# Phase one of a hybrid decoder layer: sums of squares in three groups, eps inside them, tile 1 scaled out of PSUM, tile 2's scaling ahead of tile 1's low half, constants loaded last

## The chip, the core and the metric

One core of a Trainium2 chip runs one program. The time is device microseconds (us) of one execution, and a kernel's time is the median of its runs. Differences between runs of one kernel are of the order of a per cent (the three runs of the kernel before lie between 311.09 and 315.16 us). The engines have names in the profile: PE is TensorE's matrix multiplication and PEld its weight loads, DVE is VectorE, ACT is ScalarE, POOL is GpSimd, and SP is SyncE, which issues nearly all DMAs (transfers) here.

## The reference, cut to what matters

One layer: an RMS norm of x, scaled and shifted by numbers that come from c, then a wide projection, two kinds of attention, an output projection and a gated residual. Only the first lines matter for the change:

```python
def rms_norm(x, gain):
    y = x * lax.rsqrt(jnp.mean(x * x, -1, keepdims=True) + EPS)
    return y * gain

# scale, shift, gate: c (after SiLU) @ W_ada
h = rms_norm(x) * (1 + scale) + shift      # 512 positions x 1024 features
q_a, k_a, v_a, z_a, q_b, ... = split(h @ W_in)
```

x has 512 positions (S) and 1024 features (D). EPS is 1e-6. The kernel holds x transposed, with features on the partitions: eight tiles of 128 features x 512 positions, `xT[0]` to `xT[7]`, views of one array `xTp`.

## The kernel before, in words

**Phase one** (the first 52 us of the span) makes h and multiplies it with the first 768 columns of W_in. All later phases use the same h.

*The head.* SP issues the loads in a fixed order: the eight x tiles, then for k = 0 to 3 the ada weights and the projection weights of tile k, then `rest` (constants that are first read after phase one). ACT squares each x tile as it lands (`sq`, line 347), DVE adds the squares of four tiles into one (line 349), and PE sums such a group over its partitions by a multiplication with a column of ones (`sums`, line 336: four matmuls of 128 x 128 with one column, each with a weight load of its own). There are two groups, tiles 0 to 3 and tiles 4 to 7. The four columns of `pr` in PSUM then hold the sums of squares of the 512 positions. DVE makes `sx` = sum / D + EPS from them (line 358) and `rx` = sx^(-1/2) by the classic integer trick and two Newton steps (`rsqrt`, lines 97 to 109). Four transposes on PE (line 368) turn rx into `rbp`, a tile of PSUM in which every partition holds the 512 factors, and ACT copies it to `rb` in SBUF (line 381). PE has little real work in this stage; `fillers` (line 317) are matmuls whose results are thrown away, and the table `ND` says how many stand where.

*The middle.* For tile k, `scaled` multiplies x by the factors on DVE (line 276, in place). `mod_pe`, `mod_col` and `mod_ab` (tiles 0 and 1) or `mod_rows` (tiles 2 to 7, a custom operation on DVE, line 226) make `AB`, the scale and shift of the tile's features. `h_high` on ACT makes `hh`, the high part of h, and `hf`, the whole of it (line 282; for tile 0 lines 379 and 382); `h_low` on DVE makes `hl` = hf - hh (line 285). `weights_high` on ACT and `weights_low` on DVE split the projection weights alike into `swh` (line 268) and `swl` (line 271). Then PE does `first_proj` in three passes, n = 0, 1, 2: hh with swh, hh with swl, hl with swh (lines 292 and 293). `new_tile(k)` is called in the middle of the passes of tile k - 1 and sets the order for tile k on DVE and ACT: hh and hf, the next tile's modulation, hl, the next tile's scaling, the next tile's weights.

*Order.* The order of instructions on each engine is that in which the code issues them; each engine runs its own list from front to back and waits where an input or a buffer isn't ready. Buffers rotate: `T2` hands out from a pool of 128 x 512 tiles, `sq`, `diag` and `hf` among them, and who gets a buffer waits for the last reader of its former content. `ps_pj` is a rotating pool of PSUM banks for `pr`, `pm`, `pc` and `rbp`. SP's loads of later phases are issued in the same way, when the buffers that they fill come free: at tile 4 `load_next` is called five times, which issues `w_kv_cmp` and `w_kv_sel` in halves among others.

Of the kernel before, what the change touches and what calls it, by code (L numbers as in the profile page):

```python
# [9 lines left out]
F32 = mybir.dt.float32  # L10
# [10 lines left out]
EPS = 1e-6  # L21
# [8 lines left out]
WAIT_L, WAIT_M = 4, (0, 8)  # L30
PER_A, PER_B = 3.6, (3.5, 1.6, 7)
NEAR = 256
ND = (11, (0, 0, 0, 0, 1, 1, 1, 1), (2, 0), 1, 1, 0, 3)
NR = 4
LW = 4
PE_MODS = 2
# [45 lines left out]
def hybrid_layer_kernel(ctx, tc, A, out):  # L82
# [11 lines left out]
    def T2(dt, name):  # L94
        return t2.tile([128, S], dt, name=name, tag="t2")

    def rsqrt(v, n):

        y = sm.tile([128, n], F32, name="n_y")
        t = sm.tile([128, n], F32, name="n_t")  # L100
        DVE.tensor_scalar(y.bitcast(I32), v.bitcast(I32), -0.5, float(MAGIC), op0=OP.mult, op1=OP.add)
        DVE.tensor_tensor(t, y, y, op=OP.mult)
        DVE.scalar_tensor_tensor(t, t, -0.375 * NEWTON[0], v, op0=OP.mult, op1=OP.mult)
        DVE.scalar_tensor_tensor(y, t, 0.375 * NEWTON[0] * NEWTON[1], y, op0=OP.add, op1=OP.mult)
        DVE.tensor_tensor(t, y, y, op=OP.mult)
        DVE.scalar_tensor_tensor(t, t, 64.0 / 9.0, v, op0=OP.mult, op1=OP.mult)
        DVE.scalar_tensor_tensor(t, t, -10.0 / 3.0, t, op0=OP.add, op1=OP.mult)
        DVE.scalar_tensor_tensor(y, t, 5.0, y, op0=OP.add, op1=OP.mult)
        return y
# [93 lines left out]
    def load_ada(k):  # L203
        t = ada_ring[:, k % NR]
        if k < PE_MODS:
            ada[k] = t.rearrange("p (a b c) -> p a b c", a=8, b=2)
            for e, n in ((0, 4), (4, 2), (6, 2)) if k == 0 else ((0, 4), (4, 4)):
                SP.dma_start(ada[k][:, e:e + n], A["w_ada_cols"][k][:, e:e + n])
        else:
            ada[k] = t.rearrange("p (a b) -> p a b", a=2)  # L210
            for e in range(2):
                SP.dma_start(ada[k][:, e], A["w_ada_rows"][k - PE_MODS][:, e])
# [57 lines left out]
    def weights_low(k):  # L270
        DVE.tensor_tensor(ws[k][1], wst[k], ws[k][0].bitcast(F32), op=OP.subtract)

    def scaled(k, by, parts=(slice(0, S),)):
        y[k] = xT[k]
        for c in parts:
            DVE.tensor_tensor(y[k][:, c], xT[k][:, c], by[:, c], op=OP.mult)
# [7 lines left out]
    def h_low(k):  # L284
        DVE.tensor_tensor(hl[k], hf[k], hh[k].bitcast(F32), op=OP.subtract)
# [10 lines left out]
    with in_order(tc) as begun:  # L296
# [8 lines left out]
        for k in range(NR):  # L305
# [1 line left out]
            if k == 0:  # L307
                SP.dma_start(bl, A["bias"])
            load_wst(k)
        SP.dma_start(rest, A["rest"])  # L310
        DVE.memset(scz, 0.0)


# [20 lines left out]
        def sums(acc, f, l):  # L334
            for tb in range(NB):
                PE.matmul(pr[:, tb:tb + 1], acc[:, tb * 128:(tb + 1) * 128], ones, start=f and tb == 0,
                          stop=l and tb == NB - 1, skip_group_check=True)

        for k in range(8):
            sq = stp.tile([128, S], F32, name="sacc") if k == 4 else T2(F32, "sq")  # L340
            if k % 4 == 0:
                sacc = sq
            fillers(ND[1][k], xT[k])
            if k == 4:
                sums(sacc_a, True, False)
            for n, c in enumerate(halves if k == 7 else [slice(0, S)]):
                ACT.activation(sq[:, c], xT[k][:, c], AF.Square)
                if k % 4:
                    DVE.tensor_tensor(sacc[:, c], sacc[:, c], sq[:, c], op=OP.add)
                if k == 7:  # L350
                    fillers(ND[2][n], sq[:, c])
            if k == 3:
                sacc_a = sacc
        sums(sacc, False, True)
        for e in range(2):
            ACT.activation(scrow[:, 512 * e:512 * e + 512], pj_q[e], AF.Copy)
        sx = con.tile([128, NB], F32, name="sx")
        DVE.tensor_scalar(sx, pr[:, 0:NB], 1.0 / D, EPS, op0=OP.mult, op1=OP.add)
        rx = rsqrt(sx, NB)
        DVE.tensor_scalar(prm1, prm[:, 8:16], 1.0, None, op0=OP.add)  # L360
        DVE.tensor_tensor(prmg[:, 0:8], prm1, prm[:, 24:32], op=OP.mult)
        DVE.tensor_scalar(prmg[:, 8:16], prm[:, 24:32], 0.5, None, op0=OP.mult)
# [15 lines left out]
        for c in halves:  # L378
            ACT.activation(hh[0][:, c], y[0][:, c], AF.Identity, bias=AB[:, 0, 1:2], scale=AB[:, 0, 0:1])
        ACT.copy(lsb[0:40, LINE - NEAR:LINE], pl)  # L380
        ACT.activation(rb, rbp, AF.Copy)
        ACT.activation(hf[0], y[0], AF.Identity, bias=AB[:, 0, 1:2], scale=AB[:, 0, 0:1])
        weights_low(0)
        scaled(1, rb)
        h_low(0)

        def new_tile(k):

            h_high(k, halves if k < 4 else (slice(0, S),))
            if k < 7:  # L390
                mod_rows(k + 1, (1,) if k == 1 else (0, 1))
            h_low(k)
            if k < 7:
                scaled(k + 1, rb)
                weights_high(k + 1)
                weights_low(k + 1)

        for k in range(8):
            if k + NR < 8:
                load_ada(k + NR)  # L400
                load_wst(k + NR)
            elif k == LW:
                for _ in range(5):
                    load_next()
            for n in range(3):
                first_proj(k, n)
                if k == 0 and n == 0:
# [703 lines left out]
```

## Time and profile before

| | before |
|---|---|
| median of 3 runs | 312.44 us (311.09 to 315.16) |
| profiled execution, its own time | 312.03 us |
| span of that execution | 309.4 us |
| granted TensorE clock, mean | 0.999 |
| PE, PEld busy | 302.0 us (98%), 255.2 us (82%) |
| DVE, ACT, POOL busy | 241.6 us (78%), 194.9 us (63%), 4.1 us (1%) |

The span runs from the first to the last instruction that the profiler recorded; the execution's own time is 2.6 us longer. Times in the rows below are us from the span's start, and the means of one instruction are ns. A row's bracket, such as `[0.71 <-ACT rb L381]`, says how long the engine stood idle ahead of it and which instruction ended that idle time; what stands left of `<-` in a name is the output, right of it are the inputs. A DMA row gives the kilobytes and the us from issue to landing. PE counts as busy also where it does the fillers.

### The profile page before, as it was taken

To read this page: it belongs to the slowest core of one execution; us is meant where nothing else is said; L and a number is where in the kernel's file an instruction comes from. 1 tells how busy PE (TensorE), PEld (TensorE's weight loads), DVE (VectorE), ACT (ScalarE), POOL (GpSimd) and SP (SyncE) were. 2 spreads that over 40 slices of the span, in tenths; PEclk is the share of its full clock that TensorE was granted. 3 is DMA by queue.
4 is the path that set the end of the run, shared out by engine and by line. 5 is a ranking of instruction groups with operands and counts; after the bars stand their busy time and mean duration, and the time that the engine had idled before them with its cause. 6 is when DMAs were issued, how large, how long until landed. Compare 5 with 4: busy or idle time off the path is not lost.

```text
span 309.4 us, 5849 instructions
## 1 busy us (share of the span) xinstructions
PE 302.0 (98%) x2119; PEld 255.2 (82%) x2119; DVE 241.6 (78%) x666; ACT 194.9 (63%) x472; POOL 4.1 (1%) x22
## 2 busy tenths in 40 slices
PE   8999999999999999999999999999999999999995
PEld 3678888788988999889887888888888888788885
DVE  5679998999967567898999999988789696544221
ACT  5686448668967675676936665869778877422000
POOL 0000000000000000000000000000000000000000
PEclk9999999999999999999999999999999999999999
DMA  7999969800390909170454004140420220254101
GB/s 252 382 407 408 406 202 251 307 0 0 117 328 13 293 4 263 45 271 2 154 182 158 20 2 138 65 138 3 136 71 0 68 70 2 68 172 135 68 34 68
DMA packets 28231, 44.11 MB, mean 143 GB/s; under 512 B 1787, under 2 KB 19612, under 8 KB 28204
## 3 DMA queue, kind: packets, MB, share of 16 engines
q1 hardware_dynamic: 26908, 41.57, 39.3%
q10 hardware_dynamic: 1296, 2.18, 2.3%
q8 instruction: 16, 0.26, 0.3%
q14 instruction: 11, 0.09, 0.1%
HBM read 41.61 MB, written 2.14 MB: 141 GB/s over the span
## 4 chain that ended last, share of the span: by engine, by line
PE 78%; DVE 11%; ACT 4%; DMA 3%; issue 1%; SPq 1%; DVEq 0%; ACTq 0%
PE pj L484 28%; PE po L949 8%; PE sq L292 8%; PE pj L474 8%; PE s L874 7%; PE pt L932 4%; PE skv L293 4%; PE pt L922 3%; PE s L603 3%; DVE qs L535 2%; DMA raw<-in_w_gate 2%; DVE raw L709 2%; DMA xTp<-in_xT 2%; DVE wl L177 1%; PE s L666 1%
## 5 line engine op out<-in xcount | busy, mean ns | idle before, releaser
L176 ACT ACTIVATE wh<-raw 128x512 fp32r<-128x512 f32 (+1 forms) x52 | 31.3, 635 | 18.0 <-PE pj L484 14.1
L474 PE MATMUL pj<-wl,hh 128*128 128x256 f32 (+1 forms) x128 | 36.8, 288 | 0.1
L474 PE MATMUL pj<-wh,hh 128*128 128x256 f32 (+1 forms) x128 | 37.0, 289 | 0.0
L474 PE MATMUL pj<-wh,hl 128*128 128x256 f32 (+1 forms) x128 | 36.5, 285 | 0.0
L177 DVE TENSOR_TENSOR wl<-raw,wh 128x512 fp32r<-128x512 f32 (+1 forms) x52 | 34.9, 690 | 1.8 <-ACT wh L176 1.7
L886 ACT ACTIVATE pp<-pp,nm 128x256 f32<-128x256 f32 (+2 forms) x48 | 29.3, 615 | 7.0 <-DVE nm L879 6.9
L484 PE MATMUL pj<-hl,wh 128*128 128x512 f32 x80 | 32.2, 402 | 0.0
L484 PE MATMUL pj<-hh,wl 128*128 128x512 f32 x80 | 32.0, 400 | 0.0
L484 PE MATMUL pj<-hh,wh 128*128 128x512 f32 x80 | 32.0, 400 | 0.0
L879 DVE CUSTOM_DVE_ANT_0 pp<-s,bias 128x256 f32<-128x256 f32 (+2 forms) x48 | 25.6, 553 | 4.1 <-PE s L874 3.6
L484 PE MATMUL pj<-yh,wl 128*128 128x512 f32 (+1 forms) x72 | 26.6, 370 | 0.0
L484 PE MATMUL pj<-yl,wh 128*128 128x512 f32 (+1 forms) x72 | 26.6, 369 | 0.0
L1037 DVE SCALAR_TENSOR_TENSOR fin<-pj,gate,xr 128x512 f32<-128x512 f32 (+1 forms) x9 | 6.2, 692 | 25.9 <-PE pj L484 25.9
L484 PE MATMUL pj<-yh,wh 128*128 128x512 f32 (+1 forms) x72 | 26.4, 371 | 0.0
L474 PEld LDWEIGHTS pj<-wl,hh 128*128 128x128 f32 x128 | 24.1, 188 | 0.6 <-DVE wl L177 0.3
L874 PE MATMUL s<-kTb,qs 128*128 128x256 f32 (+2 forms) x96 | 24.3, 356 | 0.0
L474 PEld LDWEIGHTS pj<-wh,hl 128*128 128x128 f32 x128 | 24.1, 188 | 0.2 <-issue 0.2
L474 PEld LDWEIGHTS pj<-wh,hh 128*128 128x128 f32 x128 | 24.1, 189 | 0.1
L907 DVE TENSOR_SCALAR pp<-pp,rr,grev 128x256 f32<-128x256 f32 (+2 forms) x48 | 21.0, 475 | 0.5
L933 ACT COPY ptT<-pt 128x384 f32<-128x384 f32 (+1 forms) x32 | 15.8, 528 | 6.0 <-PE pt L932 5.9
L534 ACT ACTIVATE qs<-pt 64x512 fp32r<-64x512 f32 x16 | 9.5, 592 | 13.4 <-PE pt L529 7.3
L484 PEld LDWEIGHTS pj<-hh,wh 128*128 128x128 f32 x80 | 15.1, 188 | 3.0 <-issue 0.2
(238 smaller groups left out, 721.4 us busy)
## 6 DMA issues: line engine op xcount, KB each, us to landing
ada_ring<-in_w_ada_rows SPq DMA_DIRECT2D x12, 512.0 KB, 7.2
raw<-in_w_cmp SPq DMA_DIRECT2D x8, 512.0 KB, 5.4
raw<-in_w_gate SPq DMA_DIRECT2D x8, 512.0 KB, 5.6
raw<-in_w_o SPq DMA_DIRECT2D x8, 512.0 KB, 4.2
wst_ring<-in_w_qkv_a SPq DMA_DIRECT2D x8, 384.0 KB, 7.7
xTp<-in_xT SPq DMA_DIRECT2D x8, 256.0 KB, 4.6
bias<-line_d SPq DMA_DIRECT2D x8, 256.0 KB, 4.1
raw<-in_w_q_b SPq DMA_DIRECT2D x4, 512.0 KB, 6.5
```

The source lines that it names most:

```text
L176: ACT.activation(wh, src, AF.Copy)
L177: DVE.tensor_tensor(wl, src, wh.bitcast(F32), op=OP.subtract)
L292: PE.matmul(pj_q[tb], lt, w[:, 0:512], start=f, stop=l, skip_group_check=True)
L293: PE.matmul(pj_kv[tb // 2][:, tb % 2, :], lt, w[:, 512:768], start=f and tb % 2 == 0, stop=l, skip_group_check=True)
L474: PE.matmul(bank[:, t * n:(t + 1) * n], h[:, tb * 128:(tb + 1) * 128], w[:, k % 2, :], start=k == 0 and m == 0, stop=k == 7 and m == 2)
L484: PE.matmul(bank, w, h[:, tok], start=k == 0 and m == 0, stop=k == 7 and m == 2)
L874: PE.matmul(ps, qs[h][:, 128 * i:128 * i + 128], k[:, hl_, lo:lo + w], start=hl_ == 0, stop=hl_ == 1)
L879: DVE.tensor_tensor_reduce(out=P[:, g, 0:w], in0=ps, in1=bt, scale=1.0, scalar=init, op0=OP.add, op1=OP.min, accum_out=nm[:, g:g + 1])
L886: ACT.activation(P[:, g, 0:e], P[:, g, 0:e], AF.Exp, bias=nm[:, g:g + 1], scale=-1.0, accum_out=dn[:, g:g + 1])
L907: DVE.tensor_scalar(v, v, rr[:, g:g + 1], gates[:, g, br:br + 1], op0=OP.mult, op1=OP.mult)
L933: ACT.copy(T[:, 0:nb, :], rev(pt[:, 0:nb * 128].rearrange("p (b q) -> p b q", b=nb)))
L949: PE.matmul(o[64 * g:64 * g + 64, 128 * i:128 * i + 128], vb[:, 64 * g:64 * g + 64], sl["T"][g][:, b, :], start=first_of and b == 0, stop= ...
```

## The change

Five things are changed, all in phase one and its loads.

1. *Groups.* The squares are summed in three groups, tiles 0 to 3, 4 and 5, 6 and 7, and PE sums each over its partitions when it is done, so there is a third call of `sums`. Each group starts in a buffer of its own.
2. *eps inside.* The addition of tile 1's squares to tile 0's also adds D * EPS / 128 to every element, which after the sum over 128 partitions is D * EPS. The step that made `sx` is gone; `rsqrt` reads `pr` in PSUM and has the factor D in its constants.
3. *Tile 1 out of PSUM.* DVE scales tile 1 by `rbp` in PSUM and no longer by `rb` in SBUF, and on ACT tile 0's `hf` goes ahead of the copy to rb.
4. *Tile 2 first.* In `new_tile(1)` tile 1's `hl` goes behind tile 2's scaling and weights.
5. *Loads and fillers.* `rest` is issued at tile 4, behind the two halves of w_kv_cmp, and no longer behind the weights of tile 3. The ada weights of tile 0 come in four pieces where there were three. The filler that stood in the middle of `mod_pe(0)` stands behind it.

```diff
--- before.py
+++ after.py
@@ -30,7 +30,7 @@
 WAIT_L, WAIT_M = 4, (0, 8)
 PER_A, PER_B = 3.6, (3.5, 1.6, 7)
 NEAR = 256
-ND = (11, (0, 0, 0, 0, 1, 1, 1, 1), (2, 0), 1, 1, 0, 3)
+ND = (11, (0, 0, 0, 0, 1, 1, 1, 1), (2, 0), 1, 0, 1, 3)
 NR = 4
 LW = 4
 PE_MODS = 2
@@ -94,16 +94,16 @@
     def T2(dt, name):
         return t2.tile([128, S], dt, name=name, tag="t2")
 
-    def rsqrt(v, n):
+    def rsqrt(v, n, times=1.0):
 
         y = sm.tile([128, n], F32, name="n_y")
         t = sm.tile([128, n], F32, name="n_t")
         DVE.tensor_scalar(y.bitcast(I32), v.bitcast(I32), -0.5, float(MAGIC), op0=OP.mult, op1=OP.add)
         DVE.tensor_tensor(t, y, y, op=OP.mult)
-        DVE.scalar_tensor_tensor(t, t, -0.375 * NEWTON[0], v, op0=OP.mult, op1=OP.mult)
-        DVE.scalar_tensor_tensor(y, t, 0.375 * NEWTON[0] * NEWTON[1], y, op0=OP.add, op1=OP.mult)
+        DVE.scalar_tensor_tensor(t, t, -0.375 * NEWTON[0] * times, v, op0=OP.mult, op1=OP.mult)
+        DVE.scalar_tensor_tensor(y, t, 0.375 * NEWTON[0] * NEWTON[1] * times, y, op0=OP.add, op1=OP.mult)
         DVE.tensor_tensor(t, y, y, op=OP.mult)
-        DVE.scalar_tensor_tensor(t, t, 64.0 / 9.0, v, op0=OP.mult, op1=OP.mult)
+        DVE.scalar_tensor_tensor(t, t, 64.0 / 9.0 / times ** 2, v, op0=OP.mult, op1=OP.mult)
         DVE.scalar_tensor_tensor(t, t, -10.0 / 3.0, t, op0=OP.add, op1=OP.mult)
         DVE.scalar_tensor_tensor(y, t, 5.0, y, op0=OP.add, op1=OP.mult)
         return y
@@ -204,7 +204,7 @@
         t = ada_ring[:, k % NR]
         if k < PE_MODS:
             ada[k] = t.rearrange("p (a b c) -> p a b c", a=8, b=2)
-            for e, n in ((0, 4), (4, 2), (6, 2)) if k == 0 else ((0, 4), (4, 4)):
+            for e, n in ((0, 2), (2, 2), (4, 2), (6, 2)) if k == 0 else ((0, 4), (4, 4)):
                 SP.dma_start(ada[k][:, e:e + n], A["w_ada_cols"][k][:, e:e + n])
         else:
             ada[k] = t.rearrange("p (a b) -> p a b", a=2)
@@ -307,7 +307,6 @@
             if k == 0:
                 SP.dma_start(bl, A["bias"])
             load_wst(k)
-        SP.dma_start(rest, A["rest"])
         DVE.memset(scz, 0.0)
 
 
@@ -336,27 +335,27 @@
                 PE.matmul(pr[:, tb:tb + 1], acc[:, tb * 128:(tb + 1) * 128], ones, start=f and tb == 0,
                           stop=l and tb == NB - 1, skip_group_check=True)
 
+        groups = []
         for k in range(8):
             sq = stp.tile([128, S], F32, name="sacc") if k == 4 else T2(F32, "sq")
-            if k % 4 == 0:
-                sacc = sq
+            if k in (0, 4, 6):
+                groups.append(sq)
+            sacc = groups[-1]
             fillers(ND[1][k], xT[k])
-            if k == 4:
-                sums(sacc_a, True, False)
+            if k in (4, 7):
+                sums(groups[k // 6], k == 4, False)
             for n, c in enumerate(halves if k == 7 else [slice(0, S)]):
                 ACT.activation(sq[:, c], xT[k][:, c], AF.Square)
-                if k % 4:
+                if k == 1:
+                    DVE.scalar_tensor_tensor(sacc, sacc, D * EPS / 128, sq, op0=OP.add, op1=OP.add)
+                elif sq is not sacc:
                     DVE.tensor_tensor(sacc[:, c], sacc[:, c], sq[:, c], op=OP.add)
                 if k == 7:
                     fillers(ND[2][n], sq[:, c])
-            if k == 3:
-                sacc_a = sacc
-        sums(sacc, False, True)
+        sums(groups[2], False, True)
         for e in range(2):
             ACT.activation(scrow[:, 512 * e:512 * e + 512], pj_q[e], AF.Copy)
-        sx = con.tile([128, NB], F32, name="sx")
-        DVE.tensor_scalar(sx, pr[:, 0:NB], 1.0 / D, EPS, op0=OP.mult, op1=OP.add)
-        rx = rsqrt(sx, NB)
+        rx = rsqrt(pr[:, 0:NB], NB, D ** 0.5)
         DVE.tensor_scalar(prm1, prm[:, 8:16], 1.0, None, op0=OP.add)
         DVE.tensor_tensor(prmg[:, 0:8], prm1, prm[:, 24:32], op=OP.mult)
         DVE.tensor_scalar(prmg[:, 8:16], prm[:, 24:32], 0.5, None, op0=OP.mult)
@@ -378,10 +377,10 @@
         for c in halves:
             ACT.activation(hh[0][:, c], y[0][:, c], AF.Identity, bias=AB[:, 0, 1:2], scale=AB[:, 0, 0:1])
         ACT.copy(lsb[0:40, LINE - NEAR:LINE], pl)
+        ACT.activation(hf[0], y[0], AF.Identity, bias=AB[:, 0, 1:2], scale=AB[:, 0, 0:1])
         ACT.activation(rb, rbp, AF.Copy)
-        ACT.activation(hf[0], y[0], AF.Identity, bias=AB[:, 0, 1:2], scale=AB[:, 0, 0:1])
         weights_low(0)
-        scaled(1, rb)
+        scaled(1, rbp)
         h_low(0)
 
         def new_tile(k):
@@ -389,19 +388,24 @@
             h_high(k, halves if k < 4 else (slice(0, S),))
             if k < 7:
                 mod_rows(k + 1, (1,) if k == 1 else (0, 1))
-            h_low(k)
+            if k > 1:
+                h_low(k)
             if k < 7:
                 scaled(k + 1, rb)
                 weights_high(k + 1)
                 weights_low(k + 1)
+            if k == 1:
+                h_low(k)
 
         for k in range(8):
             if k + NR < 8:
                 load_ada(k + NR)
                 load_wst(k + NR)
             elif k == LW:
-                for _ in range(5):
+                for n in range(5):
                     load_next()
+                    if n == 1:
+                        SP.dma_start(rest, A["rest"])
             for n in range(3):
                 first_proj(k, n)
                 if k == 0 and n == 0:
```

What the change moves on three engines follows, before and after apart. First PE in the head, from the fillers on the x tiles to the transposes of rx; `pj` stands for pr, pm and rbp, and `skv_125` is where the fillers write. Before:

```order
L317 MATMUL skv_125<-xTp 128x128
L336 MATMUL pj<-ones,sq 128x1 x4
L317 MATMUL skv_125<-xTp 128x128 x3
L317 MATMUL skv_125<-sq 128x128 x2
L336 MATMUL pj<-ones,sacc 128x1 x4
L317 LDWEIGHTS zero
L317 MATMUL skv_125<-zero 128x512
L236 MATMUL pj<-ada_ring,scz 32x256 x4
L317 LDWEIGHTS zero
L317 MATMUL skv_125<-zero 128x512
L236 MATMUL pj<-ada_ring,scz 32x256 x4
L368 MATMUL pj<-first,n_y 128x128 x4
```

The same place on PE, after:

```order
L316 MATMUL skv_125<-xTp 128x128
L335 MATMUL pj<-ones,sq 128x1 x4
L316 MATMUL skv_125<-xTp 128x128 x3
L335 MATMUL pj<-ones,sacc 128x1 x4
L316 MATMUL skv_125<-sq 128x128 x2
L335 MATMUL pj<-ones,sq 128x1 x4
L316 LDWEIGHTS zero
L316 MATMUL skv_125<-zero 128x512
L236 MATMUL pj<-ada_ring,scz 32x256 x8
L316 LDWEIGHTS zero
L316 MATMUL skv_125<-zero 128x512
L367 MATMUL pj<-first,n_y 128x128 x4
```

Four `sums` matmuls came in ahead of the two fillers on `sq`, and a filler moved from the middle of the ada matmuls (line 236) to behind them.

Second, ACT's squares of the x tiles 0 to 6 with the queues that each waits for (DMAHW: a transfer). Before:

```order
L347 ACTIVATE sq<-xTp 128x512 [waits DMAHW1_49]
L347 ACTIVATE sq<-xTp 128x512 [waits DMAHW2_49]
L347 ACTIVATE sq<-xTp 128x512 [waits DMAHW3_49]
L347 ACTIVATE sq<-xTp 128x512 [waits DMAHW4_49]
L347 ACTIVATE sacc<-xTp 128x512 [waits DMAHW5_49]
L347 ACTIVATE sq<-xTp 128x512 [waits DMAHW6_49]
L347 ACTIVATE sq<-xTp 128x512 [waits DMAHW7_49]
```

The same place on ACT, after:

```order
L348 ACTIVATE sq<-xTp 128x512 [waits DMAHW1_49]
L348 ACTIVATE sq<-xTp 128x512 [waits DMAHW2_49]
L348 ACTIVATE sq<-xTp 128x512 [waits DMAHW3_49]
L348 ACTIVATE sq<-xTp 128x512 [waits DMAHW4_49,PE_49]
L348 ACTIVATE sacc<-xTp 128x512 [waits DMAHW5_49,DVE_49,Activation_49]
L348 ACTIVATE sq<-xTp 128x512 [waits DMAHW6_49,DVE_49]
L348 ACTIVATE sq<-xTp 128x512 [waits DMAHW7_49,PE_49]
```

The squares are the same, but the buffers rotate otherwise, and four of the seven now wait for a second engine as well: tile 3's square for PE, which still reads that buffer's former content.

Third, DVE in the middle, from the scaling of tile 1 to the weights of tile 2, with its waits (`Activation` is ACT). Before:

```order
L276 TENSOR_TENSOR xTp<-xTp,rb 128x512 [waits DMAHW2_49,Activation_49]
L285 TENSOR_TENSOR hl_86<-hf,hh_78 128x512 [waits Activation_49]
L271 TENSOR_TENSOR swl<-wst_ring,swh 128x768 [waits DMAHW0_49,Activation_49]
L226 ISA ada_ring,AB<-ada_ring,scrow,first 128x1024 [waits DMAHW1_49]
L226 ISA AB 128x1
L261 TENSOR_TENSOR AB<-pj,first 128x1 [waits PE_49]
L262 SCALAR_TENSOR_TENSOR AB<-pj,prm_100,first 128x1
L226 ISA ada_ring,AB<-ada_ring,scrow,prmg 128x1024 [waits DMAHW2_49,DVE_49]
L226 ISA AB 128x1
L285 TENSOR_TENSOR hl_87<-hf,hh_79 128x512 [waits DVE_49,Activation_49]
L276 TENSOR_TENSOR xTp<-xTp,rb 128x512 [waits DMAHW3_49]
L271 TENSOR_TENSOR swl<-wst_ring,swh 128x768 [waits DMAHW3_49,Activation_49]
```

The same place on DVE, after:

```order
L276 TENSOR_TENSOR xTp<-xTp,pj 128x512 [waits DMAHW2_49,Activation_49]
L285 TENSOR_TENSOR hl_86<-hf,hh_78 128x512
L271 TENSOR_TENSOR swl<-wst_ring,swh 128x768 [waits DMAHW1_49,Activation_49]
L226 ISA ada_ring,AB<-ada_ring,scrow,first 128x1024 [waits DMAHW2_49]
L226 ISA AB 128x1
L261 TENSOR_TENSOR AB<-pj,first 128x1 [waits PE_49]
L262 SCALAR_TENSOR_TENSOR AB<-pj,prm_100,first 128x1
L226 ISA ada_ring,AB<-ada_ring,scrow,prmg 128x1024 [waits DMAHW3_49,DVE_49]
L226 ISA AB 128x1
L276 TENSOR_TENSOR xTp<-xTp,rb 128x512
L271 TENSOR_TENSOR swl<-wst_ring,swh 128x768 [waits DMAHW4_49,DVE_49,Activation_49]
L285 TENSOR_TENSOR hl_87<-hf,hh_79 128x512
```

Tile 1's scaling reads the factors from PSUM (`pj`) and still waits for ACT; the `hl` behind it, which reads `hf` from ACT, has no wait of its own any more. Tile 1's `hl` (hl_87) stands behind tile 2's scaling and weights.

## The prediction

> **What bounds the kernel now.** I read the page first, then busy times by stage (each row: stretch, its length, then busy us of PE, PEld, DVE, ACT and POOL with counts, granted clock, DMA share, GB/s), then who waits for whom in the first 52 us, then the rows of the places that the change touches.
>
> ```profile
> span 309.4 us, 5849 instructions
> 0.00:15.48 15.48, 13.60 (x74) 7.41 (x74) 9.40 (x34) 9.14 (x17) 0.76 (x6) 1.00 0.88 317
> 15.48:22.65 7.17, 7.17 (x53) 5.72 (x52) 5.52 (x10) 5.64 (x12) 0.00 (x0) 1.00 1.03 406
> 22.65:48.34 25.69, 25.69 (x143) 21.41 (x142) 24.91 (x39) 14.68 (x23) 0.00 (x0) 1.00 0.89 331
> PEld sq L292 <- DVE hl L285: 1.3, 4, 0.4
> 22.65 0.69 DVE L285 TENSOR_TENSOR hl<-hf,hh 128x512 fp32r<-128x512 f32 x1 [0.88 <-ACT hf L282]
> 24.27 0.40 PE L292 MATMUL sq<-swh,hl 128*128 128x512 f32 x1
> 28.49 0.39 PE L292 MATMUL sq<-swh,hl 128*128 128x512 f32 x1
> 37.04 0.50 PE L292 MATMUL sq<-swh,hl 128*128 128x512 f32 x1
> 45.38 0.70 DVE L285 TENSOR_TENSOR hl<-hf,hh 128x512 fp32r<-128x512 f32 x1
> 52.09 8.12 PE pj L484 x35
> 60.20 0.44 PE pt L547 x4
> ```
>
> After 52.09 the chain of waits is PE's own work (35 L484 matmuls without a pause, then L547), so what the change does to the time is what it does to the end of phase one, unless a transfer arrives late. That end hangs on DVE. From 22.65 to 48.34 DVE is busy for 24.91 of 25.69 us; PE shows no gap there, but it waits four times for `hl` (1.3 us in all), and where it doesn't wait its rounds are shorter: third passes (swh with hl) of tiles 1 and 2 start at 24.27 and 28.49, a round of 4.22, while the two from there to tile 4's (37.04) take 4.28 each. DVE's hl of tiles 1 and 6 start at 22.65 and 45.38: five rounds of 4.55. So PE catches up with DVE, and tile 6's hl (45.38 + 0.70 = 46.08) sets when PE goes into its last 52.09 - 46.08 = 6.0 us. The granted clock is 1.00 in all three stretches. The question is thus how much later or earlier DVE starts its unbroken run.
>
> **The head: squares to rx.**
>
> ```profile
> 5.57 1.88 PE L327 MATMUL sq<-diag,ones_sq 128*128 128x512 f32 x4
> L327 PE MATMUL sq<-diag,ones_sq 128*128 128x512 f32 x4 | 1.9, 592 | 0.0
> 5.35 1.37 ACT L347 ACTIVATE sq<-xTp 128x512 f32<-128x512 f32 x2 [0.31 <-DMA xTp<-in_xT]
> 7.80 2.03 ACT L347 ACTIVATE sq<-xTp 128x512 f32<-128x512 f32 x4
> 5.52 2.28 DVE L349 TENSOR_TENSOR sq<-sq 128x512 f32<-128x512 f32 x3
> 7.85 0.97 PEld L336 LDWEIGHTS pj<-ones,sq 128*128 128x128 f32 x8 [0.38 <-DVE sq L349]
> 9.57 0.52 PEld L317 LDWEIGHTS skv<-sq 128*128 128x128 f32 x4
> 10.53 0.97 PEld L336 LDWEIGHTS pj<-ones,sacc 128*128 128x128 f32 x8 [0.43 <-DVE sacc L349]
> 10.53 1.05 PE L336 MATMUL pj<-ones,sacc 128*128 128x1 f32 x8 [0.24 <-DVE sacc L349]
> 11.62 0.16 DVE L358 TENSOR_SCALAR sx<-pj 128x4 f32<-128x4 f32 x1 [0.81 <-PE pj L336]
> 11.82 0.17 DVE L101 TENSOR_SCALAR n_y<-sx 128x4 int32<-128x4 int32 x1
> 14.83 1.09 ACT L379 ACTIVATE hh<-xTp,AB 128x256 fp32r<-128x256 f32 x2 [0.37 <-DVE AB L262]
> ```
>
> Tile 3's square gets a wait for PE, which must have read the first diag (the first L327 product, two of the four matmuls in the row). The four follow each other every (1.88 - 0.59)/3 = 0.43 us, so the first product ends at 5.57 + 0.43 + 0.59 = 6.59. The two squares from 5.35 to 6.72 last 0.63 to 0.69 each, so tile 3's started near 6.06; now it starts near 6.63 and ends near 7.27, 0.55 later. Queued behind it on ACT are the other squares, whose tile landed late anyway (tile 4's began after an idle time, at 7.12), so they lose 0.15 only. The last of the three additions, which ended at 7.80, would start at 7.30 and end at 7.99. First `sums` then at 8.04, before 7.85: +0.19.
>
> From there PE's weight loads stand one after another, (0.97 - 0.19)/7 = 0.111 us apart, and nothing lies between: 8 of group one, 6 of the fillers on x, **8 new ones of group two**, 4 of the fillers on the squares make 26 x 0.111 = 2.89, so the last group starts at 10.93. Before, it started at 10.53, after 0.43 of idle time waiting for DVE: the new loads first fill that hole, and only the rest shows. DVE isn't the bound now, since group three needs one addition (tile 7's) where there were three: ACT's last square ended at 9.83 and ends about 0.15 later, and half a tile's addition behind it is done near 10.4. The sums end 0.40 later, at 11.98. What goes is `sx`: 11.82 - 11.62 = 0.20. So **rx and all that follows start 0.20 later**; without the square's wait it would be 0.0. The filler moved out of `mod_pe(0)` lets the ada product end earlier, but mod_col stands behind the transposes, which need rx: worth nothing. More pieces of ada weights: one DMA issue more on SP, its data not needed before that: nothing. hh of tile 0, at 14.83, moves to 15.03.
>
> **The middle: tile 1 out of PSUM, tile 2 ahead of tile 1's low half** (times as before, the 0.20 comes on top).
>
> ```profile
> 16.08 0.59 ACT L381 ACTIVATE rb<-pj 128x512 f32<-128x512 f32 x1
> 16.57 0.81 ACT L382 ACTIVATE hf<-xTp,AB 128x512 f32<-128x512 f32 x1
> 17.28 0.83 ACT L268 ACTIVATE swh<-wst_ring 128x768 fp32r<-128x768 f32 x1
> 21.54 1.08 ACT L282 ACTIVATE hf<-xTp,AB 128x256 f32<-128x256 f32 x2
> 22.52 0.83 ACT L268 ACTIVATE swh<-wst_ring 128x768 fp32r<-128x768 f32 x1
> 16.70 0.69 DVE L276 TENSOR_TENSOR xTp<-xTp,rb 128x512 f32<-128x512 f32 x1 [0.71 <-ACT rb L381]
> 17.41 0.69 DVE L285 TENSOR_TENSOR hl<-hf,hh 128x512 fp32r<-128x512 f32 x1
> 18.14 0.96 DVE L271 TENSOR_TENSOR swl<-wst_ring,swh 128x768 fp32r<-128x768 f32 x1
> 19.02 1.28 DVE L226 CUSTOM_DVE_ANT_0 ada_ring<-ada_ring,scrow,first 128x1024 f32<-128x1024 f32 x1
> 20.42 1.33 DVE L226 CUSTOM_DVE_ANT_0 ada_ring<-ada_ring,scrow,prmg 128x1024 f32<-128x1024 f32 x1
> 23.26 0.69 DVE L276 TENSOR_TENSOR xTp<-xTp,rb 128x512 f32<-128x512 f32 x1
> 23.86 0.95 DVE L271 TENSOR_TENSOR swl<-wst_ring,swh 128x768 fp32r<-128x768 f32 x1
> 24.73 1.28 DVE L226 CUSTOM_DVE_ANT_0 ada_ring<-ada_ring,scrow,first 128x1024 f32<-128x1024 f32 x1
> ```
>
> Before, tile 1's scaling starts at 16.70 because rb is done (0.71 of idle time ends there). The change is to free it of rb, but in the order of the changed kernel this scaling still waits for ACT, and the hl behind it has lost its own wait for ACT though it reads hf. That fits one reading only: ACT's rb copy and DVE's scaling read the same PSUM tile, the scaling is held until ACT's rb is through, and since hf stands ahead of rb now, hl is covered by the same wait. So hf takes rb's place (16.08 to 16.89), rb goes from 16.79 to 17.38 (ACT's instructions begin 0.10 ahead of the recorded end of the last), and the scaling starts at 17.41, not 16.70: **+0.71**. hl, which waited for hf before, follows 0.61 later (hl to scaling, 22.65 to 23.26) at 18.02, swl 0.60 behind it at 18.62 (ACT's swh for it still ends at 18.11). Before 18.14: +0.48, and what hangs on it gets that too: the modulation at 19.02 and 20.42, AB, and tile 1's hf (21.54 + 1.08 ends at 23.10 now) and swh of tile 2 (22.52, ends at 23.83).
>
> Here moving hl pays: DVE no longer sits for 0.88 waiting for hf, and does tile 2's scaling near 22.3. But swl of tile 2 needs that swh, and comes at 23.86 as before. Tile 1's hl, which used to be done by then, goes behind it at 24.73 and takes 0.61, so the next modulation starts at 25.34 where it started at 24.73: **+0.61**. From there DVE has no idle time up to tile 7, so all of it reaches tile 6's hl. PE gets tile 1's hl at 25.42, where its third pass began at 24.27: it stands for 1.15 us, but with rounds of 4.2 it would be at tile 6's third pass by 25.42 + 5 x 4.2 = 46.4, and DVE's hl is there at 46.08 + 0.61 = 46.7. DVE sets the end.
>
> [...]
>
> **The loads.**
>
> ```profile
> rest<-in_rest SPq DMA_DIRECT2D x1, 481.0 KB, 8.2
> raw<-in_w_kv_cmp SPq DMA_DIRECT2D x2, 512.0 KB, 9.8
> 51.35 0.22 DVE L422 TENSOR_TENSOR kg<-rest 128x64 f32<-128x64 f32 x1
> ```
>
> `rest` gives 481 KB back to a stretch where the DMA share is 1.03, but nothing on DVE, ACT or PE waits there for a transfer that it delays, so that gain is 0. In the new place it stands on SP behind a wait for PE (as read from the order, up to tile 4's third pass: 37.04 + 4.2/3 + 0.8, some 39.3), lands 8.2 later near 47.5, and is first read at 51.35 + 0.8 = 52.2: 4.6 us to spare, 3 even with the 9.8 us of w_kv_cmp. The w_kv_sel behind it waits for its buffers anyway. Cost 0.
>
> **The sum.** +0.20 and +0.61 make +0.81. On the profiled execution's own time, 312.03 (span 309.4 and 2.6 around it), that is 312.84; on the median of the runs shown, 312.44, it is 313.25. I take **313.1**, as the two frames differ by 0.4. Bounds of what the trace doesn't show: tile 3's wait between 0 and 0.20; the PSUM reads of rsqrt and scaling between -0.1 and +0.3 (sx out of PSUM took 0.16, its neighbour out of SBUF 0.17: I take 0); DVE's offset not passed on (0) or PE's 1.15 passed on whole (+1.35 in all). That makes 312.0 to 313.8 about the frames.
>
> **Rivals.**
>
> *It works as meant* (22%). The scaling isn't held by rb and runs beside ACT's hf. Then hl goes at 17.41 and everything to 21.75 as before; the scaling of tile 2 fills the idle time, swl comes when swh is done (23.35) at 23.38, hl at 24.25, the modulation at 24.86: +0.13. In the head, if PE's new loads run into the idle time and tile 3's square is not held, sums end as before and sx is saved: the best is -0.43 - 0.20 = -0.63. Together -0.5: 311.5 to 311.9. For it: the idle times 0.71, 0.88 and 0.43 are there to be taken. Against it: the waits in the order.
>
> *rest comes late* (6%, the other side). The point is 52.2: rest must land within 12.9 us of its issue. If it lands behind both halves of w_kv_cmp, 9.8 + 8.2 = 18 us, DVE's kg starts at 57.3, 5 us late, with all of DVE's work on keys and queries behind it. PE has 8.12 us of L484 before L547 needs it, so between nothing and 5 us reach PE: 313 to 318; with half of it 315.7. Against it: 8.2 us for this very load in the fuller stretch.
>
> [...]
>
> **Chances and range.** My forecast 62%, as meant 22%, rest late 6%, dearer reads 5%, 5% for what I don't see. The range, 311.1 to 315.0, takes in the forecast's bounds with the scatter of the runs, the rival as meant, and the lower half of a late rest. 2% either way, about what a measurement of this kernel can tell from no change, is 306.2 and 318.7: faster by that 1%, the same 97%, slower 2%.
>
> **What will show it.** Right: DVE's L276 of tile 1 starts as ACT's rb ends, near 17.6, behind hf; no idle time of 0.88 ahead of the hl; the first sums near 8.04 and no idle time of 0.43 ahead of the last; PE waiting about 1 us for tile 1's hl; L484 starting near 52.9; rest landing before 49. Wrong: the scaling starting beside hf; DVE idle in tiles 3 to 6, where the offset would be eaten up; a wait of kg for DMA; any of the early loads landing at other times than before, since they set the squares.

## The result, and the profile after

The changed kernel takes 313.52 us (median of 22 runs, 312.95 to 317.0), the kernel before 312.07 us (22 runs, 310.69 to 316.73). The ratio is 1.0067, with a 95% interval of 1.0044 to 1.009: slower by 0.7%. Forecast was 313.1, +0.8 us; the ratio makes it +2.1 us (1.4 to 2.8), the two medians alone +1.45. In some executions of every kernel here PE's mean granted clock is 0.995 or less (in profiles of such executions it stands at 0.50 for 3.4 to 10.3 us, from about 11 us on), so spans below are medians of the executions whose mean clock is 0.998 or more: 309.4 to 309.6 before (in each of four comparisons), 311.2 after. The profiled execution of the changed kernel took 313.45 us.

```profile
span 311.4 us, 5887 instructions
53.75 8.15 PE pj L488 x35
61.90 0.44 PE pt L551 x4
```

The first row is the page's, the other two are from the chain of waits. PE's work behind phase one starts at 53.75, where it started at 52.09, and lasts 8.15 us (8.12 before). So 1.66 of the 2.0 us by which the span grew arise in phase one. Next, who waits for whom in the first 53 us (total, times, longest):

```profile
ACT sq L348 <- PE sq L326: 1.5, 1, 1.5
DVE xTp L276 <- ACT rb L381: 1.5, 1, 1.5
DVE swl L271 <- ACT swh L268: 1.1, 1, 1.1
PEld sq L292 <- DVE hl L285: 1.2, 2, 1.1
```

The first and the third wait are new. The scaling's wait for rb was 0.7 us before, and PE's longest wait for `hl` was 0.4. The head, by the timeline of ACT, PEld, PE and DVE:

```profile
5.89 2.25 PE L326 MATMUL sq<-diag,ones_sq 128*128 128x512 f32 x4
7.33 0.63 ACT L348 ACTIVATE sq<-xTp 128x512 f32<-128x512 f32 x1 [1.54 <-PE sq L326]
8.73 0.97 PEld L335 LDWEIGHTS pj<-ones,sq 128*128 128x128 f32 x8 [0.56 <-DVE sq L352]
10.29 0.97 PEld L335 LDWEIGHTS pj<-ones,sacc 128*128 128x128 f32 x8
11.63 0.97 PEld L335 LDWEIGHTS pj<-ones,sq 128*128 128x128 f32 x8
12.73 0.16 DVE L101 TENSOR_SCALAR n_y<-pj 128x4 int32<-128x4 int32 x1 [2.12 <-PE pj L335]
14.10 0.16 DVE L108 SCALAR_TENSOR_TENSOR n_y<-n_t,n_y 128x4 f32<-128x4 f32 x1
15.79 1.09 ACT L378 ACTIVATE hh<-xTp,AB 128x256 fp32r<-128x256 f32 x2 [0.67 <-DVE AB L262]
```

Tile 3's square stands 1.54 us waiting for the diag product and starts at 7.33, not at 6.63. The first sums start at 8.73 (7.85 before). From there to the last group it is 2.90 us without a gap, as worked out (26 loads of 0.111). rsqrt starts at 12.73, 0.91 later than before. Its eight steps last 0.16 us as before and take 1.37 us from first to last start (1.39 before), so reading the sums out of PSUM costs nothing that these rows show. Now the middle, ACT's rows, then DVE's:

```profile
17.04 0.81 ACT L380 ACTIVATE hf<-xTp,AB 128x512 f32<-128x512 f32 x1
17.76 0.57 ACT L381 ACTIVATE rb<-pj 128x512 f32<-128x512 f32 x1
24.01 0.83 ACT L268 ACTIVATE swh<-wst_ring 128x768 fp32r<-128x768 f32 x1
18.37 0.69 DVE L276 TENSOR_TENSOR xTp<-xTp,pj 128x512 f32<-128x512 f32 x1 [1.48 <-ACT rb L381]
23.10 0.69 DVE L276 TENSOR_TENSOR xTp<-xTp,rb 128x512 f32<-128x512 f32 x1
24.88 0.96 DVE L271 TENSOR_TENSOR swl<-wst_ring,swh 128x768 fp32r<-128x768 f32 x1 [1.08 <-ACT swh L268]
25.75 0.69 DVE L285 TENSOR_TENSOR hl<-hf,hh 128x512 fp32r<-128x512 f32 x1
26.35 1.28 DVE L226 CUSTOM_DVE_ANT_0 ada_ring<-ada_ring,scrow,first 128x1024 f32<-128x1024 f32 x1
26.49 0.50 PE L292 MATMUL sq<-swh,hl 128*128 128x512 f32 x1 [0.73 <-DVE hl L285]
47.01 0.69 DVE L285 TENSOR_TENSOR hl<-hf,hh 128x512 fp32r<-128x512 f32 x1
47.76 0.51 PE L292 MATMUL sq<-swh,hl 128*128 128x512 f32 x1
```

Tile 1's scaling reads PSUM and still starts 0.04 us behind the end of rb. Tile 2's scaling fills idle time (23.10), but its swl then stands 1.08 us for swh. From tile 0's hh to the modulation of tile 3 it is 26.35 - 15.79 = 10.56 us; before it was 24.73 - 14.83 = 9.90. These 0.66 and the head's 0.9 (hh: +0.96) are there unchanged in tile 6's hl, 47.01 against 45.38.

### The profile page after: what moved, and what is told of

The parts are those of the page before. It is cut to its first block, busy times and chain, and to the rows that moved or that the text cites. A ratio compares the mean times of both kernels' runs of the same rounds, so it can differ in the third digit from the quotient of the medians.

```text
span 311.4 us, 5887 instructions
## 1 busy us (share of the span) xinstructions
PE 303.4 (97%) x2127; PEld 256.6 (82%) x2127; DVE 241.2 (77%) x664; ACT 194.8 (63%) x472; POOL 4.3 (1%) x22
## 4 chain that ended last, share of the span: by engine, by line
PE 81%; DVE 7%; DMA 6%; ACT 2%; issue 1%; SPq 0%; POOL 0%; DVEq 0%; ACTq 0%; POOLq 0%
PE pj L488 33%; PE pj L478 9%; PE s L878 8%; PE po L953 8%; PE sq L292 6%; PE pt L936 4%; PE pt L926 4%; PE skv L293 3%; DMA wst_ring<-in_w_qkv_a 3%; PE s L607 3%; DMA ada_ring<-in_w_ada_cols 2%; DVE qs L539 2%; DVE kTb L557 1%; DMA xTp<-in_xT 1%; PE s L670 1%
## 5 line engine op out<-in xcount | busy, mean ns | idle before, releaser
L883 DVE CUSTOM_DVE_ANT_0 pa<-s,bias,nsink 128x256 f32<-128x256 f32 (+1 forms) x32 | 14.3, 448 | 4.2 <-POOL pa L887 2.4
```

Source lines behind the costliest of these rows:

```text
L883: DVE.tensor_tensor_reduce(out=P[:, g, 0:w], in0=ps, in1=bt, scale=1.0, scalar=init, op0=OP.add, op1=OP.min, accum_out=nm[:, g:g + 1])
```

## The experiments

**The head.** Why tile 3's square waits for PE is not in the code. The section on the change puts it down to buffers that rotate, but the pool of T2 has 40 tiles (`NT2`), and tile 3's square is the 22nd that is asked for, so no rotation gives it a used one. What is left is the placement of tiles in memory: the square has been given bytes that the first diag (one of the two matrices, made from c, that PE multiplies at line 326) holds, and starts as its product ends. No run shows addresses; that it hangs on how long other tiles live, here on the late load of `rest`, is what the first experiment tests. It undoes that move.

```
+        SP.dma_start(rest, A["rest"])      # behind tile 3's weights
...
-                    if n == 1:
-                        SP.dma_start(rest, A["rest"])
```

> The changed kernel with the load of rest back in its old place. The memory is then laid out otherwise, and no square of an x tile waits for PE any more. Theory A (the head lost 0.9 us because tile 3's square waits for PE's diag product, whose buffer it got when rest moved away): first sums near 7.9 instead of 8.73, rsqrt's first step near 11.9 to 12.1 instead of 12.73, phase one ending near 53.0 instead of 53.75, time some 0.7 us below the changed kernel. Rival B (the third group's weight loads on PE cost it): rsqrt's first step stays near 12.7, time as the changed kernel. [...]

Ratio to before 1.0048 (1.0017 to 1.0078), span 310.4: 0.8 us less than the changed kernel. ACT and PEld in the head of this version:

```profile
6.26 0.63 ACT L349 ACTIVATE sq<-xTp 128x512 f32<-128x512 f32 x1 [0.52 <-DMA xTp<-in_xT]
7.93 0.97 PEld L336 LDWEIGHTS pj<-ones,sq 128*128 128x128 f32 x8 [0.53 <-DVE sq L353]
10.82 1.59 PEld L336 LDWEIGHTS pj<-ones,sq 128*128 128x128 f32 x8
```

The square waits for its own tile, the first sums start at 7.93, and all three groups' loads still follow without a gap (2.89 us to the last). The last row lasts longer, and rsqrt starts at 12.54, because the clock halves at 11.1 in this execution; at full clock, as in the rows of the changed kernel, rsqrt would come 1.10 us behind 10.82, at 11.9 by this estimate. The diag product ended early in this execution (6.25), so its rows alone would show little of the wait; the spans at full clock show it. So theory A holds for the 0.8 us. Rival B isn't out for the rest: the last sums start at 10.82 where they started at 10.53, of which eps gives back 0.20, and the span is still 1.0 above before, 0.66 of it from the middle. How the other 0.3 is made up is not shown.

The second leaves rest late and gives tile 3's square a tile of another pool.

```
-sq = stp.tile(..., name="sacc") if k == 4 else T2(F32, "sq")
+sq = stp.tile(..., name=f"own{k}") if k in (3, 4) else T2(F32, "sq")
```

> The changed kernel, but tile 3's square has a buffer of its own (as tile 4's has); rest stays late. Theory A: as with rest early, the first sums come near 7.9 to 8.1, rsqrt's first step near 12.0, phase one 0.7 us sooner than in the changed kernel, time -0.7 us. Rival B (three groups) and rival D (moving rest itself costs, by its transfer): no gain, rsqrt near 12.7 or the same end of phase one.

> The changed kernel with a buffer of its own for tile 3's square, once more, since its time was left open. Theory A (the head's 0.65 to 0.9 us is the wait for the diag product): first sums near 7.9 to 8.1 and rsqrt near 11.9 to 12.1, modulation of tile 3 still 10.56 us behind tile 0's hh, time -0.6 to -0.8 us against the changed kernel, as with rest early. Rival E (PE's own late end of the diag products, not the square's wait, sets the first sums): first sums near 8.3 to 8.5, gain 0.3 us or less.

A miss: ratios 1.0102 (1.0065 to 1.0138) and 1.006 (1.0022 to 1.0098), span 311.2 in the second (six executions), no gain. PE and ACT in the head of the second:

```profile
3.76 2.34 PE L316 MATMUL skv<-zero 128*128 128x512 bf16 x5
8.52 0.63 ACT L348 ACTIVATE own<-xTp 128x512 f32<-128x512 f32 x1 [1.71 <-PE sq L326]
```

Tile 3's square is free now, but tile 4's waits for the last diag product, until 8.52. All of them read `ones_sq`, so tile 4's own tile seems to lie on its bytes; addresses are not shown here either. The edit moved the wait by one tile, and theory A isn't tested by it. It does bear on rival E, by a later row of PE:

```profile
8.48 0.95 PE L335 MATMUL pj<-ones,sq 128*128 128x1 f32 x8
```

The first sums start at 8.48 without idle time ahead of them, as rival E says (8.3 to 8.5). Where the diag products end late, PE itself comes late to the sums. In the changed kernel's profile PE's weight loads also stood idle for 0.56 us ahead of 8.73, waiting for the squares. Without that they would have started at 8.17, which is still 0.32 later than before. So the wait of the square is the larger part of the delay there, and PE's own lateness the rest.

The third makes this wait alone: the kernel before, with tile 3's square written into the first diag.

```
-sq = stp.tile(..., name="sacc") if k == 4 else T2(F32, "sq")
+sq = stp.tile(..., name="sacc") if k == 4 else dg[0] if k == 3 else T2(F32, "sq")
```

> The kernel before with one thing changed: tile 3's square is written into the first diag's buffer, so it waits for PE's first diag product; two groups, rest early, all else as before. Theory A (this wait is the head's loss): first sums start 0.2 us later than before at the least (8.04) and 0.9 later at the most (8.7), and the time goes up by as much less the 0.4 us of slack that PE has ahead of its last sums: +0.0 to +0.5. Rival B (three groups cost it): no change in time, since the idle time ahead of the last sums takes it all.

Ratio 1.0045 (1.0009 to 1.0081), span 309.9 (six executions) where before has 309.5: within the +0.0 to +0.5 expected, but from six executions not to be told from rival B's no change. The profiled execution shows how little the wait can be (PE, then ACT):

```profile
3.76 1.30 PE L317 MATMUL skv<-zero 128*128 128x512 bf16 x5
6.20 0.63 ACT L349 ACTIVATE diag<-xTp 128x512 f32<-128x512 f32 x1 [0.57 <-PE sq L329]
```

Five fillers take 1.30 us here; the version before this has 2.34 for the same five. PE is through with the first diag product at 6.16, and the square starts at 6.20, 0.14 behind the 6.06 that the prediction has for before.

The changed kernel once more, without an edit:

> The changed kernel itself, once more, beside the next three on one chip. If the head's loss is systematic (tile 3's square waits for the diag product in every execution), the first sums start near 8.7 and rsqrt near 12.7 as in the first profile. [...]

Ratio 1.0088 (1.0055 to 1.0121), span 311.2. The wait is there again, 0.26 shorter:

```profile
7.07 0.63 ACT L348 ACTIVATE sq<-xTp 128x512 f32<-128x512 f32 x1 [1.28 <-PE sq L326]
12.47 0.16 DVE L101 TENSOR_SCALAR n_y<-pj 128x4 int32<-128x4 int32 x1 [2.00 <-PE pj L335]
26.10 1.28 DVE L226 CUSTOM_DVE_ANT_0 ada_ring<-ada_ring,scrow,first 128x1024 f32<-128x1024 f32 x1
```

rsqrt is 0.65 later than before here, 0.91 in the first profile, so the loss is no accident of one execution, but its size varies; tile 0's hh started at 15.54, and the modulation of tile 3 is again 10.56 behind it.

**The middle.** The fourth puts ACT's copy ahead of hf again and leaves the scaling out of PSUM.

```
+        ACT.activation(rb, rbp, AF.Copy)
         ACT.activation(hf[0], y[0], AF.Identity, ...)
-        ACT.activation(rb, rbp, AF.Copy)
```

> The changed kernel with ACT's copy to rb ahead of tile 0's hf again; tile 1 is still scaled out of PSUM. Theory (the scaling waits for the rb copy, so hf ahead of it costs 0.71 us): scaling of tile 1 starts 0.03 us after rb and 1.85 us after hh of tile 0 starts, as before the change, instead of 2.58; the modulation of tile 3 0.5 us sooner relative to hh; time -0.5 us against the changed kernel. Rival (the read out of PSUM itself is what costs, or hf was the one waited for): no gain, or hl then waits as much longer for hf and nothing is won.

Ratio 1.0065 (1.0034 to 1.0097), span 310.5: 0.7 less than the changed kernel, where 0.5 was expected. ACT's and DVE's rows:

```profile
16.46 1.09 ACT L378 ACTIVATE hh<-xTp,AB 128x256 fp32r<-128x256 f32 x2 [0.62 <-DVE AB L262]
17.71 0.59 ACT L380 ACTIVATE rb<-pj 128x512 f32<-128x512 f32 x1
18.33 0.69 DVE L276 TENSOR_TENSOR xTp<-xTp,pj 128x512 f32<-128x512 f32 x1 [0.77 <-ACT rb L380]
26.55 1.28 DVE L226 CUSTOM_DVE_ANT_0 ada_ring<-ada_ring,scrow,first 128x1024 f32<-128x1024 f32 x1
```

The scaling follows rb, 1.87 us behind hh (1.87 before, 2.58 in the changed kernel), and the modulation of tile 3 comes 10.09 behind hh, 0.47 sooner. What is waited for is rb; the read out of PSUM lasts 0.69, as out of SBUF.

The fifth undoes the order of tile 1's hl.

```
-            if k > 1:
-                h_low(k)
+            h_low(k)
             if k < 7:
                 ...
-            if k == 1:
-                h_low(k)
```

> The changed kernel with tile 1's hl ahead of tile 2's scaling again. Theory (in the changed kernel swl of tile 2 waits for its swh on ACT, so the new order wins nothing): idle time of 0.88 us returns ahead of hl, that of 1.08 ahead of swl goes, the modulation of tile 3 comes 0.1 to 0.2 us sooner relative to hh of tile 0, PE doesn't stand for tile 1's hl; time the same within 0.2 us, rather sooner. Rival (the new order does what it is for, filling the idle time): 0.3 us or more slower.

Ratio 1.0048 (1.0009 to 1.0087), span 310.4: 0.8 us less, not 0.2. The reason is not the order. With the other lifetimes the placement changes again, and ACT's row shows that the wait for PE is gone from the head:

```profile
6.75 0.63 ACT L348 ACTIVATE sq<-xTp 128x512 f32<-128x512 f32 x1 [0.57 <-DMA xTp<-in_xT]
```

The first experiment, which takes away this wait and keeps the order, gained the same 0.8, so little of it is left for the order. How much was not measured. And since rest stays late in this version, its transfer (rival D) can't be what cost the 0.8.

**Each gain alone.** The kernel before with eps inside, and nothing else:

```
-                if k % 4:
+                if k == 1:
+                    DVE.scalar_tensor_tensor(sacc, sacc, D * EPS / 128, sq, op0=OP.add, op1=OP.add)
+                elif k % 4:
...
-        rx = rsqrt(sx, NB)
+        rx = rsqrt(pr[:, 0:NB], NB, D ** 0.5)
```

> The kernel before with eps inside the sums and rsqrt reading PSUM, nothing else. Theory: the step sx goes, rsqrt starts 0.20 us sooner, its eight steps are as long as before (1.4 us from the first start to the last), time -0.2 us, within what can be measured. [...]

Ratio 0.9983 (0.9966 to 0.9999), span 309.2: 0.3 us less than before where 0.2 was expected, at the edge of what these runs can tell. PEld and DVE:

```profile
8.17 0.97 PEld L336 LDWEIGHTS pj<-ones,sq 128*128 128x128 f32 x8
10.41 0.97 PEld L336 LDWEIGHTS pj<-ones,sacc 128*128 128x128 f32 x8 [0.15 <-DVE sacc L351]
11.50 0.16 DVE L101 TENSOR_SCALAR n_y<-pj 128x4 int32<-128x4 int32 x1 [0.81 <-PE pj L336]
```

The first sums are late here too (8.17), because PE is, with no idle time ahead of them. The idle time ahead of the last sums takes it up (0.15 is left of 0.43): with two groups the head has that slack, with three it has none.

Then the early scaling, in a version with rest early, two groups, eps, hf ahead of rb and these lines:

```
         scaled(0, rbp, halves[1:])
+        scaled(1, rbp)
         rb = stp.tile([128, S], F32, name="rb")
...
-                    weights_low(1)
                     mod_rows(2, (0,))
+                    weights_low(1)
...
                 scaled(k + 1, rb)
+                if k == 1:
+                    h_low(k)
                 weights_high(k + 1)
```

> A version meant to be faster. rest early, two groups, eps inside; tile 1's scaling out of PSUM is issued ahead of ACT's rb copy and of tile 0's swl, so that it needs no wait for ACT; hf ahead of rb on ACT; tile 2's first modulation ahead of tile 1's swl; and for tile 1 the order scaling of tile 2, hl, swl of tile 2. Theory: the head wins 0.2 (no sx), the idle times of 0.71 and 0.88 us on DVE go for the most part, the modulation of tile 3 starts 9.1 to 9.3 us behind tile 0's hh instead of 9.9 before and 10.56 in the changed kernel; phase one ends 0.7 to 0.9 us sooner than before; time about 311.0 where the kernel before has 311.9. Rival (PE sets phase one as soon as DVE is faster, or PE's ada product of tile 1 waits for the later rb copy): no more than 0.3 us faster than before.

Ratio 1.001 (0.9986 to 1.0035), span 309.7: no gain, the rival's case. But the scaling does run at once, in one row with tile 0's second half, ahead of ACT's rb (DVE, ACT):

```profile
16.89 1.01 DVE L276 TENSOR_TENSOR xTp<-xTp,pj 128x256 f32<-128x256 f32 x2
18.98 0.58 ACT L383 ACTIVATE rb<-pj 128x512 f32<-128x512 f32 x1
```

So in these runs it is the order of issue on the shared tile that holds the second reader. ACT's copy, which is second here, starts at 18.98, well behind the scaling's end at 17.90, since ACT has `hf` ahead of it; that the copy can lose time to the scaling is not shown. Where the gain went in this version stays open.

Last, eps inside and only the place of hl, between tile 2's scaling and its swl; and the same with the early scaling, ACT's order as before:

```
+                if k == 1:
+                    h_low(k)        # behind scaled(2), ahead of weights_low(2)
```

> The kernel before with eps inside, and for tile 1 the order scaling of tile 2, hl, swl of tile 2 (hl between, where the changed kernel has it behind both). Theory: DVE does the scaling in the 0.88 us in which it waited for hf, hl follows at once, swl of tile 2 starts as its swh ends; the modulation of tile 3 starts 9.4 us behind tile 0's hh (9.9 before), phase one ends 0.5 us sooner from this and 0.2 from eps; time -0.6 to -0.7 us against the kernel before. Rival (PE's own rounds set the end of phase one as soon as DVE is faster): -0.2 us, as with eps alone, and PE shows no wait for hl in tiles 4 to 6.

> The version with eps inside and tile 1's hl between tile 2's scaling and swl, once more, since its profile fell into an execution with PE's clock halved in the middle. Theory: with the clock at 1.00 DVE's idle time ahead of hl shrinks from 0.88 to 0.3 us, the modulation of tile 3 starts 9.4 us behind tile 0's hh (9.9 before), no wait for its transfer, and tile 6's hl is 0.5 us sooner relative to hh; time 0.4 to 0.6 us below the kernel before. Rival (PE's rounds): the modulation comes as said, but PE goes through tiles 2 to 6 in rounds of 4.2 us without waiting for hl, and the end of phase one moves by 0.3 us or less.

> The same with tile 1's scaling out of PSUM ahead of tile 0's swl and ahead of ACT's rb (which keeps its place ahead of hf), and tile 2's first modulation ahead of tile 1's swl. Theory: the scaling starts right behind tile 0's, without a wait for ACT, though it reads the same PSUM tile; DVE's idle time of 0.71 goes; but tile 1's AB still waits for PE's product, so tile 2's second modulation comes 0.2 us sooner only, the modulation of tile 3 9.2 to 9.3 us behind tile 0's hh; time 0.1 to 0.2 us below the version before this. Rival (ACT's rb copy has to wait for the scaling now, and PE's ada product of tile 1 for rb): no gain or a loss of up to 0.3 us.

The place of hl with eps: ratios 0.9961 (0.9925 to 0.9997) and 0.9959 (0.9923 to 0.9995), the fastest here, below both kernels. ACT's and DVE's rows of the second:

```profile
15.95 1.09 ACT L379 ACTIVATE hh<-xTp,AB 128x256 fp32r<-128x256 f32 x2 [0.28 <-DVE AB L262]
23.77 0.69 DVE L285 TENSOR_TENSOR hl<-hf,hh 128x512 fp32r<-128x512 f32 x1 [0.29 <-ACT hf L282]
25.38 1.28 DVE L226 CUSTOM_DVE_ANT_0 ada_ring<-ada_ring,scrow,first 128x1024 f32<-128x1024 f32 x1
```

The idle time ahead of hl is 0.29 (0.88 before), and the modulation of tile 3 starts 9.43 behind hh (9.90 before, 9.4 expected). PE's work behind phase one starts 52.73 - 15.95 = 36.78 behind hh (37.26 before), so this gain reaches the end, and PE's rounds don't set it. Span 308.8, 0.7 less than before, in the second; 309.4 against 309.6 in the first. With the early scaling: 0.9967 (0.9928 to 1.0006), modulation 24.81 - 15.17 = 9.64 behind hh, no gain over it. There tile 2's first modulation stood until 18.69 for its weights to land, and tile 1's AB came behind swl.

## Why the prediction was right or wrong, by its steps

*What bounds it* was right: the offset of DVE at tile 3 reached the end of phase one. PE stood 1.1 us for tile 1's hl, went through tiles 2 to 6 in rounds of 4.2, and met DVE's hl at tile 6, which ended at 47.70 (46.7 forecast, without the head's shift); PE's third pass started at 47.76. PE's weight loads stood 0.18 us for it, so at this tile the two are nearly even (46.4 was forecast for PE).

*The middle*, +0.61, measured +0.66: right in the mechanism (rb holds the scaling, hf ahead of rb costs 0.71; the copy put back gives 0.47) and in the reason why the move of hl pays little (swl of tile 2 waits for swh). The reading that ACT's copy holds the second reader of rbp agrees with the runs as far as they go: the scaling waits where it is issued behind the copy (it starts 0.04 and 0.03 us behind its end) and runs at once where it is issued ahead (16.89, the copy at 18.98). Why two reads of one PSUM tile go one after the other is not shown.

*The head* is the step that failed in size: +0.20 forecast, +0.65 and +0.91 measured. The forecast (tile 3's square near 6.63, the first sums at 8.04) took the diag product's end, 6.59, from the one execution of before. There nobody on ACT waited for it, so the profile gave no sign of how much it varies: it ended at 7.29 and 7.04 in the two profiles of after, where PE came to it at 5.89 behind its fillers, and not at 5.57. The working itself was right. The version with the copy put back has the same head and the same wait, and in its profile the diag product ended at 6.45 (ACT, PEld, DVE):

```profile
6.49 0.63 ACT L348 ACTIVATE sq<-xTp 128x512 f32<-128x512 f32 x1 [0.68 <-PE sq L326]
7.97 0.97 PEld L335 LDWEIGHTS pj<-ones,sq 128*128 128x128 f32 x8 [0.64 <-DVE sq L352]
12.00 0.16 DVE L101 TENSOR_SCALAR n_y<-pj 128x4 int32<-128x4 int32 x1 [1.63 <-PE pj L335]
```

The first sums start at 7.97, and rsqrt comes 0.18 later than before. Where the product ends late, the square's wait grows and PE comes late to the first sums. With loads that leave no slack behind the first sums, each such delay reaches rsqrt in full. The forecast's bound for this wait, 0 to 0.20, was drawn from the same single execution and was too narrow. That it hangs on the placement of tiles, which the load of rest sets off, was not seen either.

*The loads*: rest was issued at 40.90 and landed in 3.6 us, not 8.2; kg, its first reader, started at 52.97 without a wait for it. As forecast, its transfer costs nothing.

```profile
rest<-in_rest SPq DMA_DIRECT2D x1, 481.0 KB, 3.6
52.97 0.22 DVE L426 TENSOR_TENSOR kg<-rest 128x64 f32<-128x64 f32 x1
```

*The rivals* fell: the scaling's idle time grew from 0.71 to 1.48 us where the version that works as meant would lose it, and rest came early. No run shows a dearer PSUM read, to which the forecast gives 5% and, among its bounds, up to +0.3: reads out of PSUM lasted the same 0.16 and 0.69 us as those out of SBUF.

*The sum* was +0.81; the first profile shows +1.66 in phase one, the spans at full clock differ by 1.7. That the time itself came within half a us of the forecast was partly luck: the forecast started from 312.03 and 312.44 us, the latter the median of three runs, and 22 runs put the kernel before at 312.07. From there +0.81 would have been 312.88. The 0.3 us that the span grew behind phase one (311.4 - 53.75 against 309.4 - 52.09) isn't accounted for.

## What to carry to other kernels

A change of lifetimes (a load moved, an operand kept longer) can move buffers that the change never names, so look in the order for waits that engines have gained. Price such a wait by the slack behind it and by how far the thing waited for varies, not by one execution. In this kernel, a second reader of a PSUM tile started sooner only where it was issued ahead of the first: DVE's scaling at 16.89, ACT's copy at 18.98; issued behind the copy, the scaling stood until 0.04 and 0.03 us after the copy's end.

## What the runs showed of the hardware

PE's granted clock was halved in stretches that begin at different times of the kernel and differ in length. The stretches in which the granted clock was below 1.00, from two versions (stretch, its length, busy us, clock, DMA share, GB/s): the copy put back first, then rest early.

```profile
11.00:12.00 1.00, 1.00 (x11) 0.90 (x9) 0.00 (x1) 0.00 (x0) 0.00 (x0) 0.88 1.03 399
15.00:16.00 1.00, 1.00 (x10) 0.97 (x8) 0.26 (x1) 0.84 (x2) 0.00 (x0) 0.91 1.03 408
11.00:12.00 1.00, 1.00 (x8) 1.00 (x7) 0.00 (x0) 0.00 (x0) 0.00 (x0) 0.54 1.06 393
20.00:22.00 2.00, 2.00 (x14) 1.40 (x17) 2.00 (x4) 0.49 (x1) 0.00 (x0) 0.67 1.06 415
```

With 0.50 in between, the first is at half clock from 11.76 to 15.18, 3.42 us, the second from 11.08 to 21.32, 10.24, three times as long. In the profile of the wait alone it lasts from 10.68 to 17.52 (0.84 in 10.00:11.00, 0.62 in 16.00:18.00), 6.84, twice as long. What sets the start and the length is not shown. PE's pace varies before that too: the five fillers take 1.30 us in the wait alone and 2.34 in the version with a buffer of its own, and in the profile of before the same filler lasts from 0.63 us down to 0.38 while the granted clock's record reads 1.00. The cause is not shown either. In six profiles the half clock and the start of the diag products go together: where they start at 5.07 (the wait alone) or 5.17 (hl between, the second run), the half clock came later, and where they start at 5.57 (before) or 5.89 (the changed kernel twice, the own buffer's second run), it did not. In these six, then, the executions at full clock are those in which the diag product comes late (it ended at 6.59 in before and at 7.29 and 7.04 in the changed kernel, at 6.16 in the wait alone), which is when the changed kernel's new wait costs most. Of the other eight profiles no such start is given here.
